# Input norm in two token halves, each followed by half of the first projection; the second layer reloads the transposed memory from DRAM

## The chip, the cores and the metric

The kernel runs on one core of one Trainium2 chip. The metric is device time in microseconds, median of three runs. Engines in the rows below: PE is TensorE (matmul), PEld its weight loads, DVE is VectorE, ACT is ScalarE, POOL is GpSimd, SP is SyncE, which issues most DMAs.

## The reference, cut to what matters

All of it is float32. `D_MODEL` is 1024, `SEQ` 512, `BATCH` 1, `DEPTH` 2, 256 memory tokens.

```python
def reference(x, mem, ln0_g, ln0_b, ...):
    h = layer_norm(x, ln0_g, ln0_b)                      # the input norm
    for l in range(DEPTH):
        mix = hybrid_mixer(h, w_in[l], ...)
        h = layer_norm(DEEPNORM_ALPHA * h + mix, ln1_g[l], ln1_b[l])
        xa = memory_cross_attention(h, mem, w_xq[l], w_xkv[l], w_xo[l])
        h = layer_norm(DEEPNORM_ALPHA * h + xa, ln2_g[l], ln2_b[l])
        ff = swiglu(h, w_ffn_in[l], w_ffn_out[l])
        h = layer_norm(DEEPNORM_ALPHA * h + ff, ln3_g[l], ln3_b[l])
    return h

def hybrid_mixer(h, w_in, ...):
    proj = h @ w_in                                      # c_a, c_g, q, k, v, r, a_low
    u = c_a * sigmoid(c_g)
    u = silu(layer_norm(causal_depthwise_conv(u, conv_w, conv_b), conv_ln_g, conv_ln_b))   # 31 taps
    ...
def memory_cross_attention(x, mem, w_q, w_kv, w_o):
    kv = mem @ w_kv                                      # mem: 256 x 1024, the same in both layers
    ...
```

## The kernel before, in words

A float32 operand is held as two fp32r tiles, a high part and the rest: `split` (L101) writes the high part with an ACT copy and the rest with a subtraction on DVE or POOL. `mm3` (L147) multiplies two such pairs with three matmuls (L148, L149, L150). Weights come in chunks of 512 KB: `wchunk` (L130) issues the load on SP into one of four `raw` buffers, then splits it into one of four `w` buffers (the ring). `wlo_engines` says which engine does the subtraction. After each such load, `behind` pops one waiting piece of work off the list `aside` and has it issued right after that load; before the change only `weight_sums`, later in each layer, puts anything there.

`proj_feat` (L223) computes a projection with features on the partitions: weights stationary, tokens moving, 512 of them in one matmul, or, with `halves`, 256 of them, first all matmuls of tokens 0 to 255 and then those of tokens 256 to 511, over the same four chunks.

The program starts with the memory: `mem_T` (L609) loads `mem` in four quarters, transposes each with four PE transposes, and splits the result into `mT` (two tiles of 128 x 2048 numbers, 1 MB each). `mem_V` (L638) makes V of layer 0 from it, K follows later in `mem_K`. Then comes the input norm (L665 to L684): statistics and the inverse deviation of four tiles of 128 tokens on DVE, the normalisation of each on ACT (L677), then for each of eight feature blocks four PE transposes into one PSUM bank (tag `tr`, two banks), an ACT step `xf` with gain and bias (L683), and a split into `hT`. The first projection on `hT` is `conv_in(0)` (L796), two groups of two chunks (`raw_c`, `w_c`, banks `pp_c`); `conv_taps` (L740) then runs 31 taps per channel tile on DVE at the lowest priority, `gates` (L754) comes between, and `conv_in(1)` is the other half of the channels. `residual0` multiplies and adds the gain and bias to `h` on POOL. In layer 1, `mem_T` is called again after `conv_in(0)`, since its tiles were given up in between.

The framework plans the program when it is built: it tracks the dependencies, hands out buffers, and orders each engine's instructions by priority (program order; `high_priority(offset=HP)` moves a block ahead) against its own estimate of times. So every engine has a fixed order of its own, and what stands later in the program can fill a gap. A small change of the text can move that order elsewhere too.

```python
    aside = []

    def behind(load):
        if aside:
            with tc.issue_after(load.ins):
                aside.pop(0)()
```

Of the kernel before, what the change touches and what calls it, by code (L numbers as in the profile page):

```python
# [12 lines left out]
F32 = mybir.dt.float32  # L13
# [38 lines left out]
def trunk(ctx: ExitStack, tc, a, out):  # L52
# [15 lines left out]
    def f(ap):  # L68
        return ap.bitcast(F32)
# [536 lines left out]
            dest.first(j, sg, uu)  # L606


    def mem_T(name):  # L609

        mT = [block([P, NK, MEM], F32R, f"mT{j}_{name}") for j in range(2)]
        mraws = block([P, 2, D], F32, f"mem_{name}")

        def part(*quarters):
            for mt, i in quarters:
                cs = slice(i * 512, i * 512 + 512)
                nc.sync.dma_start(mraws[:, mt, cs], a["mem"][0, mt * P:(mt + 1) * P, cs])
            for mt, i in quarters:
                pt = bank(f"mt{mt}{i}_{name}", tag="tr")
                for k in range(4):  # L620
                    PE.transpose(pt[:, k * P:(k + 1) * P], mraws[:, mt, (i * 4 + k) * P:(i * 4 + k + 1) * P], ident)
                ks, ms_ = slice(i * 4, i * 4 + 4), slice(mt * P, (mt + 1) * P)
                split(mT[0][:, ks, ms_], mT[1][:, ks, ms_], pt.rearrange("p (k t) -> p k t", k=4))

        return lambda kt: (mT[0][:, kt, :], mT[1][:, kt, :]), part

    def new_K(l):
        return [block([P, NK, MEM], F32R, f"KT{j}_{l}") for j in range(2)]
# [16 lines left out]
        for tt in tts:  # L645
            nc.sync.dma_start(h[tt], a["x"][0, tt * P:(tt + 1) * P, :])

    mT, mem_part = mem_T("0")
    mem_part((0, 0))
    lnrow = const.tile([2 * NK, P], F32, name="lnrow")  # L650
    V = new_V(0)
# [10 lines left out]
    DVE.tensor_copy(lncol, pl[:, :2 * NK])  # L662
    KT = new_K(0)
    hT = new_hT("ln0")
    with tc.high_priority(offset=HP):  # L665
        for tt in range(NT):
            st = ln_stats(tt, "ln0")
            for i in range(2):
                DVE.bn_stats(st[:, i, :], h[tt][:, i * 512:(i + 1) * 512])
            mv = small.tile([P, 2], F32, tag="mv", name=f"mv_ln0{tt}")  # L670
            DVE.bn_aggr(mv, st)
            v0 = small.tile([P, 1], F32, tag="v", name=f"v_ln0{tt}")
            DVE.tensor_scalar(v0, mv[:, 1:2], EPS, VS, ALU.add, ALU.mult)
            y0 = rstd_of(v0, 1, f"ln0{tt}")
            b0 = small.tile([P, 1], F32, tag="b0", name=f"b_ln0{tt}")
            DVE.scalar_tensor_tensor(b0, mv[:, 0:1], -1.0, y0, ALU.mult, ALU.mult)
            ACT.activation(h[tt], h[tt], AF.Identity, scale=y0, bias=b0)  # L677
        for k in range(NK):
            pt = bank(f"lt_ln0_{k}", tag="tr")
            for tt in range(NT):  # L680
                PE.transpose(pt[:, tt * P:(tt + 1) * P], h[tt][:, k * P:(k + 1) * P], ident)
            xf = tmp.tile([P, T], F32, tag="t", name=f"xf{k}")
            ACT.activation(xf, pt, AF.Identity, scale=lncol[:, k:k + 1], bias=lncol[:, NK + k:NK + k + 1])  # L683
            split(hT[0][k // 4][:, k % 4, :], hT[1][k // 4][:, k % 4, :], xf)  # L684

    gb0 = []

# [11 lines left out]
    for l in range(L):  # L699
# [30 lines left out]
        def conv_in(half):  # L730
            def ev_g(m, ps):
                ACT.activation(u[:, half * 2 + m, :], ps, AF.Sigmoid)

            def ev_a(m, ps):
                DVE.tensor_mul(u[:, half * 2 + m, :], u[:, half * 2 + m, :], ps)

            proj_feat(w_in, mov, [(CD + half * 256, 256, ev_g), (half * 256, 256, ev_a)], n_(f"c{half}"),
                      halves=half == 0 and l > 0)

        def conv_taps(half):  # L740
            cts = range(half * 2, half * 2 + 2)
# [12 lines left out]
        def gates():  # L754
# [38 lines left out]
            ACT.activation(kd, kd, AF.Exp, scale=1.0 / TAU)  # L793
            DVE.tensor_copy(dec, qe[:, :, CH - 1::CH])

        conv_in(0)  # L796
        if l == 0:
            residual0(0, 1)
        wlo_engines(POOL)
        if l > 0:  # L800
            mT, mem_part = mem_T(f"{l}")
            mem_part((0, 0), (1, 0), (0, 1), (1, 1))
            KT = new_K(l)
        conv_taps(0)
        gates()
# [288 lines left out]
```

## Time and profile before

| what | us |
|---|---|
| median of 3 runs | 1412.63 (1412.57 to 1413.6) |
| the profiled execution, its own time | 1414.95 |
| its span, first to last instruction | 1413.3 |
| around the span | 1.65 |

The profile is one execution. Durations below come from it, and a sum is made against its 1414.95 us, which is 2.32 us above the median. Matmuls are pipelined: the time from one start to the next is what PE needs, the duration shown is longer.

### The profile page before, as it was taken

The numbers are of one execution on the slowest core, as the hardware profiler recorded it, in microseconds if no ns is written. First come the engines' busy times: TensorE is split into PE (matmuls) and PEld (weight loads), VectorE is DVE, ScalarE is ACT, GpSimd is POOL, SyncE is SP. The second block draws the span as 40 slices with busy tenths as digits, with TensorE's granted clock in tenths as the row PEclk, the third lists the DMA queues.
The fourth block names the chain that finished last, engine by engine and source line by source line (L and its number), as shares of the span: only waits on it lengthen the run. The fifth ranks groups of instructions, "written<-read, shape, count | busy, mean of one in ns | idle before, by whom it ended". The sixth has DMA issues, their size and how long they took to land.

```text
span 1413.3 us, 22464 instructions
## 1 busy us (share of the span) xinstructions
PE 1380.2 (98%) x8847; PEld 1235.4 (87%) x8847; DVE 1110.4 (79%) x1905; ACT 650.4 (46%) x1065; POOL 181.8 (13%) x130
## 2 busy tenths in 40 slices
PE   7998999999999999999999999999999999999997
PEld 6687888988899899989888889889889998998996
DVE  6599978656988878877768999685579887878767
ACT  5652361343366456545235336524425653664550
POOL 2373331110000000001003300011100000000000
PEclk9999999999999999999999999999999999999998
DMA  7512247796255675565333225659913747646641
GB/s 255 154 60 87 93 148 196 203 259 164 75 134 142 193 174 150 165 193 134 122 111 103 75 90 179 227 140 275 223 60 107 180 136 204 176 138 204 154 134 60
DMA packets 131197, 214.79 MB, mean 152 GB/s; under 512 B 8956, under 2 KB 83408, under 8 KB 131092
## 3 DMA queue, kind: packets, MB, share of 16 engines
q1 hardware_dynamic: 118388, 175.35, 38.0%
q0 software_dynamic: 12416, 37.75, 14.6%
q8 instruction: 69, 1.13, 0.3%
q14 instruction: 36, 0.29, 0.1%
q10 hardware_dynamic: 288, 0.26, 0.1%
HBM read 190.27 MB, written 35.65 MB: 160 GB/s over the span
## 4 chain that ended last, share of the span: by engine, by line
PE 87%; DVE 3%; ACT 3%; issue 3%; POOL 2%; DMA 1%; SPq 0%; DVEq 0%; ACTq 0%; POOLq 0%
PE fx L551 5%; PE fx L553 5%; PE fx L552 5%; PE fw L553 3%; PE fw L552 3%; PE fw L551 3%; PE pp_xq L149 2%; PE pp_xq L148 2%; PE pp_xq L150 2%; PE foX_fo L512 2%; PE po_xo L150 2%; PE po_xo L148 2%; PE foX_fo L513 2%; PE po_xo L149 2%; PE foX_fo L514 2%
## 5 line engine op out<-in xcount | busy, mean ns | idle before, releaser
L750 DVE SCALAR_TENSOR_TENSOR cv<-u,chan,cv 128x511 f32<-128x511 f32 (+29 forms) x240 | 159.6, 728 | 0.2
L103 DVE TENSOR_TENSOR w_s<-s,w_s 128x1024 fp32r<-128x1024 f32 x80 | 97.6, 1220 | 38.9 <-ACT w_s L102 38.7
L306 POOL DMA_DIRECT2D s<-raw_a x40 | 34.8, 881 | 627.3 <-DVE h L495 187.1
L102 ACT ACTIVATE w_s<-s 128x1024 fp32r<-128x1024 f32 x80 | 84.5, 1056 | 66.5 <-DMA s<-raw_a 36.3
L551 PE MATMUL fx<-T_ln,w_s 128*128 128x256 f32 x320 | 90.6, 284 | 0.5 <-ACT u L564 0.5
L553 PE MATMUL fx<-T_ln,w_s 128*128 128x256 f32 x320 | 90.5, 283 | 0.0
L552 PE MATMUL fx<-T_ln,w_s 128*128 128x256 f32 x320 | 90.5, 283 | 0.0
L102 ACT ACTIVATE w_a<-raw_a 128x1024 fp32r<-128x1024 f32 x60 | 63.2, 1056 | 32.4 <-PE foX_fo L514 13.1
L103 DVE TENSOR_TENSOR w_a<-raw_a,w_a 128x1024 fp32r<-128x1024 f32 x60 | 73.1, 1219 | 5.0 <-ACT w_a L102 4.7
L551 PEld LDWEIGHTS fx<-T_ln,w_s 128*128 128x128 f32 x320 | 61.4, 192 | 0.9 <-ACT u L564 0.9
L552 PEld LDWEIGHTS fx<-T_ln,w_s 128*128 128x128 f32 x320 | 61.4, 192 | 0.0
L553 PEld LDWEIGHTS fx<-T_ln,w_s 128*128 128x128 f32 x320 | 61.4, 192 | 0.0
L149 PE MATMUL pp_xq<-hT_ln,w_xq 128*128 128x256 f32 (+1 forms) x192 | 61.3, 322 | 0.0
L148 PE MATMUL pp_xq<-hT_ln,w_xq 128*128 128x256 f32 (+1 forms) x192 | 59.9, 320 | 0.5 <-ACT hT_ln L102 0.5
L150 PE MATMUL pp_xq<-hT_ln,w_xq 128*128 128x256 f32 (+1 forms) x192 | 60.4, 318 | 0.0
L102 ACT ACTIVATE hT_ln<-lt_ln 128x512 fp32r<-128x512 f32 x24 | 13.9, 595 | 97.5 <-PE lt_ln L215 97.3
L149 PE MATMUL pp_c<-hT_ln,w_c 128*128 128x512 f32 (+1 forms) x160 | 56.9, 358 | 0.2 <-DVE hT_ln L103 0.2
L148 PE MATMUL pp_c<-hT_ln,w_c 128*128 128x512 f32 (+1 forms) x160 | 55.1, 361 | 1.7 <-DVE h L295 1.5
L150 PE MATMUL pp_c<-hT_ln,w_c 128*128 128x512 f32 (+1 forms) x160 | 56.3, 354 | 0.0
L102 ACT ACTIVATE w_S_fo<-raw_S_fo 128x1024 fp32r<-128x1024 f32 x32 | 33.8, 1058 | 35.8 <-PE foX_fo L514 14.2
L149 PE MATMUL po_xo<-w_xo,oTh 128*128 128x512 f32 x128 | 49.5, 389 | 0.0
L150 PE MATMUL po_xo<-w_xo,oTl 128*128 128x512 f32 x128 | 49.4, 391 | 0.0
(369 smaller groups left out, 4869.2 us busy)
## 6 DMA issues: line engine op xcount, KB each, us to landing
raw_a<-w_ffn_in SPq DMA_DIRECT2D x60, 512.0 KB, 4.1
s<-raw_a POOLq DMA_DIRECT2D x40, 512.0 KB, 5.6
raw_fo<-w_ffn_out SPq DMA_DIRECT2D x36, 512.0 KB, 3.9
S_fs<-w_ffn_out SPq DMA_DIRECT2D x32, 512.0 KB, 6.4
raw_S_fo<-S_fs SPq DMA_DIRECT2D x32, 512.0 KB, 3.7
s<-w_ffn_in SPq DMA_DIRECT2D x20, 512.0 KB, 3.4
raw_xv<-w_xkv SPq DMA_DIRECT2D x16, 512.0 KB, 5.7
raw_c<-w_in SPq DMA_DIRECT2D x16, 512.0 KB, 4.7
```

The source lines that it names most:

```text
L102: ACT.activation(hi, src, AF.Copy)
L103: eng.tensor_sub(lo, src, f(hi))
L148: PE.matmul(o, lh, rh, start=start, stop=False)
L149: PE.matmul(o, lh, rl, start=False, stop=False)
L150: PE.matmul(o, ll, rh, start=False, stop=stop)
L306: POOL.dma_start(dst, src, accum_op=ALU.add, max_dma_last_dim=4096)
L512: PE.matmul(o, ph[:, ts_], wh, start=first, stop=False, skip_group_check=True)
L513: PE.matmul(o, ph[:, ts_], wl, start=False, stop=False, skip_group_check=True)
L551: PE.matmul(o, wh, bh, start=start and k == 0, stop=False, skip_group_check=True)
L552: PE.matmul(o, wh, bl, start=False, stop=False, skip_group_check=True)
L553: PE.matmul(o, wl, bh, start=False, stop=stop and k == 3, skip_group_check=True)
L750: DVE.scalar_tensor_tensor(cv[ct][:, s:], u[:, ct, :T - s], wj, cv[ct][:, s:], ALU.mult, ALU.add)
```

## The change

The input norm becomes a function of a token half: statistics, normalisation, transposes and splits of tiles 0 and 1, then of tiles 2 and 3. A PSUM bank holds two feature blocks of 256 tokens instead of one of 512, with one `xf` step for each and one split for both. `conv_in(0)` runs in token halves in layer 0 too. In layer 0 the two `mT` tiles are written to DRAM (`mdram`), each behind one of the weight loads of `conv_in(0)`; in layer 1 two POOL DMAs read them back, in place of the loads, transposes and splits of `mem_T`.

```diff
+    mdram = [dram.tile([P, NK, MEM], F32, tag=f"mT{j}", name=f"mT{j}_dram") for j in range(2)]
+
+    def mem_views(mT):
+        return lambda kt: (mT[0][:, kt, :], mT[1][:, kt, :])
+
+    def mem_again(l):
+
+        mT = [block([P, NK, MEM], F32R, f"mT{j}_{l}") for j in range(2)]
+        for j in range(2):
+            POOL.dma_start(mT[j], mdram[j])
+        return mem_views(mT)
...
     hT = new_hT("ln0")
-    with tc.high_priority(offset=HP):
-        for tt in range(NT):
+    def input_norm(t):
+        tts = range(t * 2, t * 2 + 2)
+        for tt in tts:
             st = ln_stats(tt, "ln0")
...
             ACT.activation(h[tt], h[tt], AF.Identity, scale=y0, bias=b0)
-        for k in range(NK):
-            pt = bank(f"lt_ln0_{k}", tag="tr")
-            for tt in range(NT):
-                PE.transpose(pt[:, tt * P:(tt + 1) * P], h[tt][:, k * P:(k + 1) * P], ident)
-            xf = tmp.tile([P, T], F32, tag="t", name=f"xf{k}")
-            ACT.activation(xf, pt, AF.Identity, scale=lncol[:, k:k + 1], bias=lncol[:, NK + k:NK + k + 1])
-            split(hT[0][k // 4][:, k % 4, :], hT[1][k // 4][:, k % 4, :], xf)
+        s = slice(t * 256, t * 256 + 256)
+        for k2 in range(NK // 2):
+            pt = bank(f"lt_ln0_{t}{k2}", tag="tr")
+            xf = tmp.tile([P, T], F32, tag="t", name=f"xf{t}{k2}")
+            for e in range(2):
+                k, es = k2 * 2 + e, slice(e * 256, e * 256 + 256)
+                for i, tt in enumerate(tts):
+                    PE.transpose(pt[:, e * 256 + i * P:e * 256 + (i + 1) * P], h[tt][:, k * P:(k + 1) * P], ident)
+                ACT.activation(xf[:, es], pt[:, es], AF.Identity, scale=lncol[:, k:k + 1],
+                               bias=lncol[:, NK + k:NK + k + 1])
+            k4 = k2 * 2 % 4
+            split(hT[0][k2 // 2][:, k4:k4 + 2, s], hT[1][k2 // 2][:, k4:k4 + 2, s],
+                  xf.rearrange("p (e c) -> p e c", e=2))
+
+    with tc.high_priority(offset=HP):
+        for t in range(2):
+            input_norm(t)
...
             proj_feat(w_in, mov, [(CD + half * 256, 256, ev_g), (half * 256, 256, ev_a)], n_(f"c{half}"),
-                      halves=half == 0 and l > 0)
+                      halves=half == 0)
...
+        if l == 0:
+            for j in range(2):
+                aside.append(lambda j=j: nc.sync.dma_start(mdram[j], f(mT_tiles[j])))
         conv_in(0)
         if l == 0:
             residual0(0, 1)
         wlo_engines(POOL)
         if l > 0:
-            mT, mem_part = mem_T(f"{l}")
-            mem_part((0, 0), (1, 0), (0, 1), (1, 1))
+            mT = mem_again(l)
             KT = new_K(l)
         conv_taps(0)
```

## Rows read from the trace of the kernel before

**Rows 1.** The page: the span, and busy time, share of the span and instructions of each engine.

```profile
span 1413.3 us, 22464 instructions
PE 1380.2 (98%) x8847; PEld 1235.4 (87%) x8847; DVE 1110.4 (79%) x1905; ACT 650.4 (46%) x1065; POOL 181.8 (13%) x130
```

**Rows 2.** What PE waited for in the whole run, longest in total first: us in total, times, longest.

```profile
PE mt L621 <- DMA mem<-mem: 6.2, 2, 4.1
PE lt_ln L681 <- ACT xf L683: 3.4, 1, 3.4
PE pt_v L149 <- POOL w_v L103: 1.9, 1, 1.9
PE ogt L954 <- DVE og L950: 1.8, 1, 1.8
```

**Rows 3.** PE in order of time around the input norm and `conv_in(0)` of layer 0: start, duration, instruction, count, and in brackets the idle time before it.

```profile
35.33 0.60 PE L681 MATMUL lt_ln<-ident,h 128*128 128x128 f32 x4
39.34 1.70 PE L681 MATMUL lt_ln<-ident,h 128*128 128x128 f32 x8 [3.41 <-ACT xf L683]
40.69 2.06 PE L148 MATMUL pp_c<-hT_ln,w_c 128*128 128x512 f32 x4
42.97 0.63 PE L150 MATMUL pp_c<-hT_ln,w_c 128*128 128x512 f32 x1
43.39 0.47 PE L149 MATMUL pp_c<-hT_ln,w_c 128*128 128x512 f32 x1
...
61.57 0.39 PE L148 MATMUL pp_c<-hT_ln,w_c 128*128 128x512 f32 x1
...
66.10 0.39 PE L150 MATMUL pp_c<-hT_ln,w_c 128*128 128x512 f32 x1
66.33 3.86 PE L770 MATMUL al<-hT_ln,wa 128*32 128x512 f32 x16
```

**Rows 4.** Stretches of that time: us, PE, PEld, DVE, ACT and POOL busy, the granted clock of PE (1.00 is 2.4 GHz), the busy share of the DMA engines, GB/s.

```profile
30.00:32.00 2.00, 2.00 (x11) 1.65 (x10) 0.77 (x7) 1.82 (x2) 0.13 (x1) 1.00 0.91 261
32.00:34.00 2.00, 2.00 (x12) 1.63 (x11) 0.00 (x0) 2.00 (x3) 0.00 (x0) 1.00 1.00 339
36.00:38.00 2.00, 0.00 (x0) 0.00 (x0) 2.00 (x2) 2.00 (x3) 0.00 (x0) 1.00 0.00 0
40.00:42.00 2.00, 2.00 (x7) 1.80 (x8) 1.19 (x2) 1.38 (x2) 0.00 (x0) 0.54 0.51 80
```

**Rows 5.** ACT in order of time, from the normalisation of the four tiles on.

```profile
30.18 4.64 ACT L677 ACTIVATE h<-h,b_ln,y_ln 128x1024 f32<-128x1024 f32 x4 [4.04 <-DVE b_ln L676]
34.73 1.99 ACT L102 ACTIVATE w_c<-raw_c 128x1024 fp32r<-128x1024 f32 x2
36.62 0.57 ACT L102 ACTIVATE V<-pt_xv 128x512 fp32r<-128x512 f32 x1
37.10 1.04 ACT L102 ACTIVATE w_c<-raw_c 128x1024 fp32r<-128x1024 f32 x1
38.05 0.57 ACT L102 ACTIVATE V<-pt_xv 128x512 fp32r<-128x512 f32 x1
38.52 1.43 ACT L683 ACTIVATE xf<-lt_ln,lncol 128x512 f32<-128x512 f32 x2
```

**Rows 6.** SP in order of time: the four loads of `conv_in(0)` in layer 0.

```profile
27.75 9.68 SPq L134 DMA_DIRECT2D raw_c<-w_in  x4
```

**Rows 7.** DMA in the window 1404 to 1413 us, the last stores of the output from SBUF to DRAM: GB/s in 40 equal slices.

```profile
GB/s 0 0 0 0 0 0 0 0 0 0 0 0 0 0 46 337 391 364 383 410 355 46 0 0 0 0 114 341 223 350 342 337 332 287 5 0 0 0 0 0
```

**Rows 8.** Layer 1, PE: `conv_in(0)` in halves, and then the transposes of the memory.

```profile
724.12 0.28 PE L148 MATMUL pp_c<-hT_ln,w_c 128*128 128x256 f32 x1
...
726.88 0.29 PE L148 MATMUL pp_c<-hT_ln,w_c 128*128 128x256 f32 x1
...
745.24 1.04 PE L621 MATMUL mt<-ident,mem 128*128 128x128 f32 x8
746.04 3.96 PE L770 MATMUL al<-hT_ln,wa 128*32 128x512 f32 x16
749.83 0.40 PE L148 MATMUL pp_c<-hT_ln,w_c 128*128 128x512 f32 x1
...
752.80 0.60 PE L621 MATMUL mt<-ident,mem 128*128 128x128 f32 x4
753.16 0.47 PE L149 MATMUL pp_c<-hT_ln,w_c 128*128 128x512 f32 x1
```

**Rows 9.** PE: the transposes of the memory in both layers, and in layer 1 the first of the three lines that read `mT` for K (count; ns, least, median, most; first and last start).

```profile
L621 PE MATMUL mt<-ident,mem x32: 270/273/476, 4.1 to 754.0; 128*128 128x128 f32 x32
...
L148 PE MATMUL pp_xk<-mT,w_xk x64: 278/283/387, 818.7 to 870.7; 128*128 128x256 f32 x64
```

**Rows 10.** The tile `S_fs` in DRAM: the POOL instruction that issues a DMA of 512 KB (ns, least, median, most), and the us to landing of the DMAs that write it, from DRAM to DRAM.

```profile
L306 POOL DMA_DIRECT2D S_fs<-S_fs x16: 814/840/1372, 231.1 to 1017.7; - x16
DMA to landing us min/median/max: 3.2/8.0/9.9
```

**Rows 11.** Layer 0, POOL in order of time, behind `conv_in(0)`.

```profile
65.72 9.50 POOL L693 TENSOR_TENSOR h<-h,gb_ln 128x1024 f32<-128x1024 f32 x4
75.17 2.42 POOL L103 TENSOR_TENSOR w_c<-raw_c,w_c 128x1024 fp32r<-128x1024 f32 x1
77.53 9.48 POOL L694 TENSOR_TENSOR h<-h,gb_ln 128x1024 f32<-128x1024 f32 x4
86.98 7.10 POOL L103 TENSOR_TENSOR w_qk<-raw_qk,w_qk 128x1024 fp32r<-128x1024 f32 x3
```

**Rows 12.** DVE: one addition of `gates` in layer 0 and in layer 1; ACT: the copy of the first conv half, ahead of the `w_v` split of the wait in rows 2.

```profile
85.20 9.95 DVE L785 TENSOR_TENSOR qk<-qk 128x1024 f32<-128x1024 f32 x1 [2.50 <-ACT qk L784]
769.40 1.23 DVE L785 TENSOR_TENSOR qk<-qk 128x1024 f32<-128x1024 f32 x1 [2.96 <-ACT qk L784]
123.86 0.60 ACT L752 ACTIVATE acc<-cv 128x512 f32<-128x512 f32 x1 [13.76 <-DVE cv L750]
```

**Rows 13.** What PE waited for from 700 to 910 us, as in rows 2: the end of layer 0 and the mixer of layer 1.

```profile
PE pp_c L148 <- DVE h L295: 1.5, 1, 1.5
PE pu L839 <- DVE S L851: 0.4, 1, 0.4
```

More of the change, by code (lines that the diff above doesn't have):

```diff
@@ L623, in part @@
                 split(mT[0][:, ks, ms_], mT[1][:, ks, ms_], pt.rearrange("p (k t) -> p k t", k=4))
-        return lambda kt: (mT[0][:, kt, :], mT[1][:, kt, :]), part
+        return mT, part
     def new_K(l):
@@ L646, in load_x @@
             nc.sync.dma_start(h[tt], a["x"][0, tt * P:(tt + 1) * P, :])
-    mT, mem_part = mem_T("0")
+    mT_tiles, mem_part = mem_T("0")
+    mT = mem_views(mT_tiles)
     mem_part((0, 0))
```

## Prediction, made before the changed kernel was run

> **What bounds the kernel now.** I read the page first: PE is busy for 1380.2 of 1413.3 us [rows 1], so only two things can shorten this kernel, PE work that goes and PE idle time that goes. Then the list of PE's waits, because it says where the 33 us of idle time lie. The largest, 6.2 us, is the first load of the memory, which the change doesn't touch. The second is the one place the change aims at: 3.4 us before a transpose of the input norm, waiting for ACT's `xf` [rows 2].
>
> The order of time shows how that wait comes about. V's matmuls end at about 35.3, the eight transposes among and behind them fill both banks, and from 35.93 PE has nothing until 39.34 [rows 3]. ACT did not idle: four tile normalisations from 30.18 to 34.8, then three weight splits and two V copies, and only at 38.52 the first `xf`, which frees a bank [rows 5]. So PE waits for ACT's queue. [...] Eight transposes then took 1.35 us (39.34 to 40.69) against 0.80 us for eight at full clock in layer 1 [rows 3, 8], and the matmuls up to 43.39 came about 0.43 us apart (42.97 to 43.39), where the same form later takes 0.227 (20 intervals from 61.57 to 66.10) [rows 3]. From 40.69 to 43.39 there are 6 matmuls, so the clock cost 0.55 + 6 x 0.20 = 1.75 us.
>
> **The change part by part.**
>
> *The wait and the clock.* With the norm in halves, the first `xf` needs two tile normalisations on ACT, not four. Each takes about 1.15 us (4.64 for four, [rows 5]), and the statistics of tiles 0 and 1 no longer queue behind those of 2 and 3. The transposes of half 0 can then run while V's matmuls still last. If hT of half 0 is ready when V ends, PE goes on without a gap: 3.41 us of wait and 1.75 us of clock are gone, 5.16 in all. I don't take all of it: at 36 to 38 us ACT is busy the whole time [rows 4], and weight splits and V copies still want 5 us of it around that point [rows 5]. ACT also gets 16 `xf` steps of half the columns for 8 whole ones; a whole one takes about 0.7 (1.43 for two, [rows 5]), so 8 more cost between nothing and 5.6 us of ACT, nearer 2 if half a step saves less than half. They lie beside PE's first pass of 11.5 us. I leave 1.0 us of wait: -4.2.
>
> *The halves.* 96 matmuls of 512 tokens become 192 of 256. Layer 1 shows their pace: 724.12 to 726.88 are 23 intervals of 0.120 us [rows 8]. A pair takes 0.240 for 0.227: 96 x 0.013 = +1.3 us. The number of input transposes stays at 32, the splits at 8. The ring's four chunks are now held into the second pass. Layer 1 already works that way, and PE goes from the last half (745.24) through 16 gate matmuls to the next projection at 749.83 without a gap [rows 8]; cost 0. Head in sum: -4.2 + 1.3 = -2.9; at best -5.16 + 1.3 = -3.9, at worst +1.3 with the wait kept.
>
> *The two stores.* 2.10 MB from SBUF to DRAM on SP's queue, one behind the first and one behind the second weight load. Nothing in `mT` is late for them. Output stores move 337 to 410 GB/s in their full slices, about 370 [rows 7], so 5.7 us of DMA time; by the rate of the weight loads themselves, 261 to 339 [rows 4], 6 to 8 us. What is queued behind: chunks 2, 3 and 4 of `conv_in(0)`. Before, the first three are issued from 27.75 on and loaded by about 34 us [rows 4, 6]. With the stores between, the third lands at about 34 + 5.7 = 40 and is split some 2.2 us later (1.04 ACT [rows 5], then as much again for the subtraction): 42. PE, if it starts the first pass at 36.5, uses a chunk in 24 x 0.12 = 2.9 us and wants the third at 42.3. So it is just hidden, by the first two chunks' work. If the stores are slower, the planner has 5.8 us of second-pass work on the first two chunks to put there. I take 0.
>
> [...]
>
> *Layer 1.* Four loads of 256 KB on SP, 16 transposes, four ACT copies and four DVE subtractions go. PE: eight transposes take 745.24 to 746.04, 0.80; a group of four takes 0.36 plus about 0.08 at the change of form, twice: 0.8 + 0.9 = -1.7 us [rows 8]. From 700 to 910 us PE's largest wait is 1.5 us for the layer before, and the next 0.4 [rows 13]; nothing takes the gain back, so all of it counts. ACT's and DVE's relief is off the path: 0. In its place two POOL instructions, 0.84 us each by the nearest one [rows 10] (for 512 KB; here 1 MB, so 0.8 to 1.7 each), and 2.10 MB of reads. K, the first reader, starts at 818.7 [rows 9], over 70 us after `conv_in(0)` ends. Even 10 us to landing, the most that a DMA of that kind took [rows 10], is hidden. Behind them in POOL's queue stand the subtractions of `conv_in(1)`'s chunks; if the planner puts the reads ahead of these, they are late by 2 to 3 us against 4.6 us of gate matmuls. 0, at worst +3.
>
> *Sum:* -2.9 - 1.7 = -4.6 us. The profiled execution's 1414.95 becomes 1410.3; the median's 1412.63 becomes **1408.0**.
>
> **The rivals.**
>
> *B: the head's gain is eaten later in layer 0.* PE waits 1.9 us for `w_v` near 125.5 [rows 2]. That chunk's ACT split stands behind the copy of the first conv half, which waited 13.76 us for DVE's taps [rows 12]. The taps share DVE with one addition that took 9.95 us in layer 0 and 1.23 in layer 1; in layer 0 it ran from 85.2 to 95.15, under POOL's unbroken run that ends at 94.08 [rows 11, 12]. If POOL's run, which begins with the residual at 65.72 when its gain and bias have landed, doesn't come earlier with `conv_in(0)`, DVE is held until the same moment, the taps end at the same 123.9, and PE waits there for what it gained. Then only layer 1 counts: -1.7, 1410.9. For it: POOL is behind from 65.7 to 94 [rows 11]. Against it: that run waits for chunk splits and a load whose places in the queues move with PE.
>
> *C, slower: the stores hold the weights.* Its place is SP's queue at 28 us. The third chunk is ready at 34 + 2 stores + 2.2 and PE, after the first two chunks (42.3) and their second pass (+5.8), stands still from 48.1: it decides from 6 us a store, and since the other terms give 5.16 - 1.3 + 1.7 = 5.6 us back, the kernel is slower than before from 8.8 us a store. DMAs of 512 KB that write DRAM took 8.0 us to land in the median [rows 10], so 16 for 1 MB at the worst; at 12, the middle between that and the point where it turns, the chunk is ready at 60.2, PE stands 12.1 us, loses 1.75 to the clock again, and the sum is 12.1 + 1.75 - 5.6 = +8.3: 1420.9. For it: the loads queue behind the stores. Against it: rows 10 are DRAM to DRAM in a busy stretch, rows 7 are the direction in question, 2.8 us a store.
>
> *D: a transpose holds PE for as long as it lasts.* One lasts 0.273 us [rows 9]; 16 of them would be 4.4 us, 2.7 more than I count, and the time 1405.3. Against it: the trace starts them 0.10 us apart, since they overlap [rows 8]. [...]
>
> *E: the plan moves.* All engines' orders are planned anew. Waits like those of 1.5 to 1.9 us [rows 2] can appear or vanish anywhere in layer 0: -4 to +5 around the forecast.
>
> **How the numbers follow.** Forecast (1405 to 1410): 0.50. B (1410 to 1412.5): 0.22. C (1415.5 to 1424): 0.10. D (1405): 0.02. E on its own, outside these: 0.16, of which 0.04 below 1405, 0.06 about as before, 0.06 slower. 0.2% of 1412.6 is 2.8 us, about what a measurement here tells from no change. Faster by more: 0.50 + 0.06 + a little of B = 0.58. Within: most of B and 0.06 of E, 0.27. Slower: C and the rest of E, 0.15. For 8 in 10, the range runs from 1403.5 to 1414.5: below lies part of E's low end, above it C and part of E.
>
> **What would show it.** The wait of PE for `xf` near 36 us falls from 3.4 to about 1 us and the clock stays at 1.00 at 36 to 44 us. `conv_in(0)` ends, and the gate matmuls start, near 63 instead of 66.33. The `pp_c` matmuls of layer 0 are 256 wide and 0.120 apart. No `mt` transpose after 20 us, and K's first matmul in layer 1 comes without a wait for a DMA. B would show as a longer wait at `pt_v` with POOL's run still ending at 94; C as ACT waiting for `raw_c` at 36 to 60 us. I would be wrong most plainly if PE's idle time at the head grew.

## The result, and the profile after

The changed kernel takes 1415.61 us in the median of 21 runs (1413.72 to 1420.21), the kernel before 1413.61 in 21 runs beside them: a ratio of 1.0017, 95% interval 1.0010 to 1.0024. It is some 2.4 us slower; I had forecast 1408.0 in a range up to 1414.5. By the prediction's own 0.2% it is "within", at the edge to "slower"; "faster", which had the largest chance, did not come. The profiled execution of after took 1418.09 us, 3.1 more than that of before.

The page of after, its span and busy times, for [rows 1]:

```profile
span 1416.4 us, 22624 instructions
PE 1381.0 (98%) x8927; PEld 1241.3 (88%) x8927; DVE 1104.4 (78%) x1901; ACT 652.6 (46%) x1070; POOL 187.4 (13%) x132
```

PE's busy time grew by 0.8 us (96 more matmuls, 16 fewer transposes) and its idle time by 2.3. The list of PE's waits of after says where that is, for [rows 2]:

```profile
PE mt L633 <- DMA mem<-mem: 6.4, 2, 3.9
PE ogt L980 <- DVE og L976: 3.8, 1, 3.8
PE lt_ln L699 <- ACT xf L700: 2.9, 2, 1.7
PE po_mo L150 <- DVE cUl L103: 2.4, 2, 1.3
PE pp_qk L148 <- DVE u L759: 2.1, 1, 2.1
```

The wait for `xf`, which the change was to shorten, is 2.9 us instead of 3.4, now in two parts. The waits at `pt_v` are gone, and three have come or grown in layer 0's mixer, all three for DVE: `u` (the gated input of the convolution), `og` (the gated attention output) and `cUl` (the low part of the convolution's output, which the mixer's output projection `po_mo` reads).

**The head.** PE of after in order of time, for [rows 3]:

```profile
37.21 0.89 PE L699 MATMUL lt_ln<-ident,h 128*128 128x128 f32 x4 [1.27 <-ACT xf L700]
39.77 0.89 PE L699 MATMUL lt_ln<-ident,h 128*128 128x128 f32 x4 [1.66 <-ACT xf L700]
40.75 0.74 PE L148 MATMUL pp_c<-hT_ln,w_c 128*128 128x256 f32 x2
...
68.10 2.25 PE L794 MATMUL al<-hT_ln,wa 128*32 128x512 f32 x9
```

The first `pp_c` starts at 40.75 (before: 40.69), the gate matmuls `al` at 68.10 (before: 66.33). ACT in the same stretch, for [rows 5]:

```profile
30.63 4.65 ACT L691 ACTIVATE h<-h,b_ln,y_ln 128x1024 f32<-128x1024 f32 x4 [4.04 <-DVE b_ln L690]
35.18 1.04 ACT L102 ACTIVATE w_c<-raw_c 128x1024 fp32r<-128x1024 f32 x1
36.13 0.57 ACT L102 ACTIVATE V<-pt_xv 128x512 fp32r<-128x512 f32 x1
36.61 1.01 ACT L700 ACTIVATE xf<-lt_ln,lncol 128x256 f32<-128x256 f32 x2
37.71 1.06 ACT L102 ACTIVATE w_c<-raw_c 128x1024 fp32r<-128x1024 f32 x1
38.68 0.58 ACT L102 ACTIVATE V<-pt_xv 128x512 fp32r<-128x512 f32 x1
39.16 1.02 ACT L700 ACTIVATE xf<-lt_ln,lncol 128x256 f32<-128x256 f32 x2
40.06 0.64 ACT L102 ACTIVATE hT_ln<-xf 128x512 fp32r<-128x512 f32 x1
```

The source has two halves, ACT's queue does not: the plan put all four normalisations first, and the weight splits and V copies between the `xf` pairs. The first cast to `hT`, on which `pp_c` waits, comes at 40.06. The clock falls as it did before; stretches of after, columns as in [rows 4] (the clock as a share of full speed; no trace here gives it in GHz):

```profile
36.00:38.00 2.00, 0.77 (x4) 0.40 (x4) 1.74 (x2) 1.90 (x5) 0.00 (x0) 1.00 1.07 445
40.00:42.00 2.00, 1.90 (x10) 1.45 (x9) 1.62 (x4) 2.00 (x5) 0.00 (x0) 0.71 1.07 293
42.00:44.00 2.00, 2.00 (x11) 2.00 (x11) 0.83 (x2) 2.00 (x4) 0.00 (x0) 0.50 0.19 45
```

**Layer 1.** PE of after behind the first half of the convolution, for [rows 8]; then, for [rows 9], the memory's transposes in the whole run and the reload (count; ns, least, median, most; first and last start):

```profile
749.84 3.87 PE L794 MATMUL al<-hT_ln,wa 128*32 128x512 f32 x16
753.55 0.40 PE L148 MATMUL pp_c<-hT_ln,w_c 128*128 128x512 f32 x1
```

```profile
L633 PE MATMUL mt<-ident,mem x16: 364/421/476, 3.9 to 13.4; 128*128 128x128 f32 x16
L618 POOL DMA_DIRECT2D mT<-mT_dram x2: 552/570/587, 745.1 to 745.7; - x2
```

No transpose of the memory stands there any more, and K has no wait. After was 4.6 us behind before when layer 1 began (first `pp_c` of each trace, 720.69 against 716.11), 3.8 at `al` and 2.7 at the first `pp_qk`: 1.9 us given back. The clock falls once in this stretch in both traces (0.50 at 724 to 726 us in after, at 720 to 722 in before). e2 and e4 (below), where it does not fall there, differ by the same 1.9 us (55.5 and 53.6 us from the first `pp_c` to `pp_qk`).

Between head and layer 1 the distance to before runs like this: +1.8 at `al`, +4.0 at the end of `pp_qk` (the mixer's q and k), -2.1 at the end of `pt_v` (its v), +4.2 at the first `po_mo`, +6.7 at `pp_xq` (the first projection behind the mixer), +4.6 at the end of layer 0. So the 3.1 us between the two traces are 1.8 at the head, another 2.8 in the rest of layer 0, -1.9 in layer 1 up to `pp_qk` and 0.4 behind it. The mixer of layer 0, for which my sum had no term, decides.

### The profile page after: what moved, and what is told of

The parts are those of the page before. It is cut to its first block, busy times and chain, and to the rows that moved or that the text cites. A ratio compares the mean times of both kernels' runs of the same rounds, so it can differ in the third digit from the quotient of the medians.

```text
span 1416.4 us, 22624 instructions
## 1 busy us (share of the span) xinstructions
PE 1381.0 (98%) x8927; PEld 1241.3 (88%) x8927; DVE 1104.4 (78%) x1901; ACT 652.6 (46%) x1070; POOL 187.4 (13%) x132
## 4 chain that ended last, share of the span: by engine, by line
PE 87%; DVE 8%; ACT 2%; DMA 1%; issue 1%; SPq 0%; DVEq 0%; ACTq 0%
PE fx L551 5%; PE fx L553 5%; PE fx L552 5%; DVE cv L774 3%; PE fw L553 3%; PE fw L552 3%; PE fw L551 3%; PE pp_xq L148 2%; PE pp_xq L149 2%; PE pp_xq L150 2%; PE po_xo L150 2%; PE foX_fo L512 2%; PE foX_fo L513 2%; PE po_xo L148 2%; PE po_xo L149 2%; PE pp_c L149 2%
## 5 line engine op out<-in xcount | busy, mean ns | idle before, releaser
L774 DVE SCALAR_TENSOR_TENSOR cv<-u,chan,cv 128x511 f32<-128x511 f32 (+28 forms) x240 | 158.9, 729 | 0.1
L149 PE MATMUL pp_c<-hT_ln,w_c 128*128 128x256 f32 (+1 forms) x192 | 62.6, 329 | 0.2 <-DVE hT_ln L103 0.2
L148 PE MATMUL pp_c<-hT_ln,w_c 128*128 128x256 f32 (+1 forms) x192 | 60.8, 328 | 1.8 <-DVE h L295 1.5
L150 PE MATMUL pp_c<-hT_ln,w_c 128*128 128x256 f32 (+1 forms) x192 | 62.1, 327 | 0.0
```

Of the source, the lines that this page charges most:

```text
L148: PE.matmul(o, lh, rh, start=start, stop=False)
L149: PE.matmul(o, lh, rl, start=False, stop=False)
L150: PE.matmul(o, ll, rh, start=False, stop=stop)
L774: DVE.scalar_tensor_tensor(cv[ct][:, s:], u[:, ct, :T - s], wj, cv[ct][:, s:], ALU.mult, ALU.add)
```

## The experiments

All ratios are to the kernel before, in runs taken beside it; 0.1% is 1.4 us.

| kernel | median us | ratio (95%) |
|---|---|---|
| after | 1415.61 | 1.0017 (1.0010 to 1.0024) |
| e1 reload alone | 1410.47 | 0.9985 (0.9971 to 0.9999) |
| e2 halves alone | 1418.60 | 1.0036 (1.0025 to 1.0047) |
| e3 norm halved, projection whole | 1416.78 | 1.0028 (1.0015 to 1.0041) |
| e4 late stores | 1416.82 | 1.0025 (1.0013 to 1.0037) |
| e5 after, mixer's splits on DVE | 1410.48 | 0.9975 (0.9962 to 0.9988) |
| e6 after, half 0 first on ACT | 1417.37 | 1.0026 (1.0015 to 1.0038) |
| e7 after, gain loaded early | 1409.93 | 0.9979 (0.9969 to 0.9988) |
| e8 = e1 + e5's edit | 1407.48 | 0.9960 (0.9948 to 0.9972) |
| e9 = e6 + late stores | 1418.56 | 1.0033 (1.0020 to 1.0045) |
| e10 = e9 + e5's and e7's edits | 1410.10 | 0.9972 (0.9961 to 0.9982) |
| e11 = e1 + e5's and e7's edits | 1403.39 | 0.9925 (0.9908 to 0.9941) |
| e12 = after + e5's and e7's edits | 1408.48 | 0.9951 (0.9932 to 0.9969) |
| e13 = e9, splits behind `xf` | 1418.98 | 1.0035 (1.0022 to 1.0049) |
| e14 = e13 + e5's and e7's edits | 1407.99 | 0.9962 (0.9950 to 0.9974) |
| e15 = before + e5's and e7's edits | 1407.13 | 0.9955 (0.9940 to 0.9971) |
| e16 = e9, splits behind `hT` | 1415.94 | 1.0012 (1.0000 to 1.0024) |
| e17 = e16 + e5's and e7's edits | 1402.01 | 0.9925 (0.9909 to 0.9941) |

### Which part of the change costs

e1 is the kernel before with the stores and the reload; e2 the changed kernel with layer 1's transposes back and no stores; e3 and e4 are the changed kernel with one edit each:

```diff
 e3:
-                      halves=half == 0)
+                      halves=half == 0 and l > 0)
 e4 (the two stores, queued ahead of conv_in(1) instead of conv_in(0)):
+        gates()
+        if l == 0:
+            for j in range(2):
+                aside.append(lambda j=j: nc.sync.dma_start(mdram[j], f(mT_tiles[j])))
         conv_in(1)
```

> The kernel before with the second half of the change alone: the two stores behind the loads of conv_in(0) in layer 0 and the reload in layer 1; input norm and conv_in(0) as before. Theory 1 (layer 1 gains its 1.7 us, and what the change loses is lost in layer 0 by the halves): about 1.9 us faster than before, with conv_in(0) of layer 0 ending at the same 66 us. Theory 2 (the stores hold the weights of conv_in(0)): ACT waits for raw_c, conv_in(0) ends 2 us or more later, and the whole is at the time of before or up to 3 us slower.

> The changed kernel without stores and reload: layer 1 transposes the memory again. Theory 1 (the halves cost layer 0 some 4 us): about 4 us slower than before, 1417 to 1418. Theory 2 (the stores do): conv_in(0) starts earlier than 40.7 us and ends before 66 us, and the whole is 0 to 3 us faster than before.

> The changed kernel with one part undone: conv_in(0) of layer 0 runs over all 512 tokens at once again, the input norm stays in halves. If the 256 wide matmuls are the loss at the head (96 pairs of 0.240 for 0.227 us), conv_in(0) ends 1.3 us earlier than in the changed kernel and the whole is about 1.3 us faster than it. If the halves of the projection are what lets PE start, PE waits longer before conv_in(0) (its first matmul then needs both halves of hT), and the whole is slower than the changed kernel by 3 us or more.

> The changed kernel with the two stores behind the first two loads of conv_in(1) instead of conv_in(0). If the stores hold the weights of conv_in(0), its last two chunks come 3 to 6 us earlier, and conv_in(0) ends 1 to 3 us earlier than 68.1. If ACT's queue alone sets the start, conv_in(0) ends at 68 as before and the time stays within 1 us of the changed kernel.

The reload brings 2.1 us (0.1 to 4.1), the halves cost 5.1 (3.5 to 6.6); 0.9985 x 1.0036 = 1.0021, the change's 1.0017 within the intervals. So the loss is the halves'. In e3 the first `pp_c` starts 6.3 us later than in before and `al` 4.9 later: the halved projection does let PE start while half 1 is not there, but that only makes good what the halved norm alone would cost. In e4 `al` comes 3.0 us later than in before, against 1.8 in after: moving the stores away did not bring the head forward, and rival C falls. These distances hold a part that is the clock's: at the head it was at half from 40.1 to 43.6 us in before (0.50 at 41 to 43), twice as long in e4 and three times as long in e3, in part while PE waited.

### What holds the mixer of layer 0

The chain of work that ended last runs in after, from 90 to 149 us, almost wholly over DVE: the gates' steps and the convolution's taps. In before it runs from 80 to 128 us over POOL: the residual, then the splits of `w_qk` and `w_v`, with gaps between them. Two stretches (columns as in [rows 4]), first before, then e17:

```profile
90.00:110.00 20.00, 20.00 (x89) 16.33 (x88) 20.00 (x23) 7.16 (x8) 10.85 (x5) 1.00 0.39 117
110.00:150.00 40.00, 36.30 (x205) 29.92 (x204) 39.99 (x65) 11.46 (x17) 16.20 (x8) 0.96 0.32 99
```

```profile
90.00:110.00 20.00, 20.00 (x90) 16.57 (x89) 20.00 (x30) 7.10 (x7) 8.94 (x5) 1.00 0.36 110
110.00:150.00 40.00, 40.00 (x246) 33.31 (x245) 39.96 (x69) 14.10 (x19) 18.05 (x8) 1.00 0.35 106
```

The columns are, after the window's length, PE, PEld, DVE, ACT, POOL: in before DVE is busy for 20.00 of 20 and 39.99 of 40 us. That alone does not hold PE. In e17 DVE is as busy, and so is PE, for all of the 60 us: the taps have the lowest priority and fill what DVE has left. What holds PE is a single DVE step that comes late when PE needs its result. And DVE's busy time is not all work. DVE of after, from the gates on, and POOL beside it:

```profile
90.08 1.97 DVE L809 TENSOR_TENSOR qk<-qk 128x1024 f32<-128x1024 f32 x1 [3.96 <-ACT qk L808]
93.27 5.39 DVE L811 TENSOR_TENSOR_SCAN dk<-reset,qk 128x512 f32<-128x512 f32 x2
99.85 2.09 DVE L815 TENSOR_TENSOR dk<-dk 128x1024 f32<-128x1024 f32 x1
101.86 0.68 DVE L759 TENSOR_TENSOR u<-u,pp_c 128x512 f32<-128x512 f32 x1
```

```profile
88.54 2.44 POOL L103 TENSOR_TENSOR w_qk<-raw_qk,w_qk 128x1024 fp32r<-128x1024 f32 x1
90.91 3.40 POOL L718 TENSOR_TENSOR h<-h,gb_ln 128x1024 f32<-128x1024 f32 x1
94.27 6.59 POOL L103 TENSOR_TENSOR w_qk<-raw_qk,w_qk 128x1024 fp32r<-128x1024 f32 x2
```

The addition takes 1.97 us where it takes 1.23 undisturbed [rows 12]: it starts at 90.08, POOL's split ends at 91, and it is done 1.1 us later. So the last of the three: POOL's splits end at 100.86, and it too is done 1.1 us later. The two scans between them also end 1.1 us after the POOL step in which each began (95.39 after 94.31, 98.66 after 97.58). The taps between these steps, which add up in a PSUM bank, keep their 0.73 us beside the same POOL work. Why the one kind of step waits for POOL and the other does not, no trace here shows. `u` frees the bank that `pp_qk` waits for.

The wait for `og` is of this kind too, and here before and after differ in what was held. In after two small DVE steps ahead of `og` stood beside POOL splits, from 177.74 to 180.15 and from 182.33 to 184.28 us; in before only the first did, and the wait was 1.8 us instead of 3.8. During the longer wait the clock fell, and it is at half from 184 to 191 us in after (0.51 in the mean).

e5 takes POOL's part in the mixer's second group of splits away, e7 makes POOL's run earlier (`gb0` holds the gain and bias of the residual):

```diff
 e5:
         if l == 0:
-            wlo_engines(POOL, DVE)
+            wlo_engines(DVE)
 e7:
+        if l == 0:
+            gb0.append(load_gb(a["ln0_g"], a["ln0_b"], "ln0"))
         conv_in(0)
```

> The changed kernel, where from the second chunk pair of K in layer 0 on (up to the output projection of the mixer) all weight subtractions are done by DVE, not by POOL and DVE in turn. Theory H (a DVE instruction that reads and writes only SBUF stands still while a POOL instruction runs, and that is what the mixer's end loses): the waits for cUl and cUh before po_mo (3.6 us) and for og (3.8 us) shrink to 2 us or less together, and the whole is 3 to 5 us faster than the changed kernel. Theory O (the loss there is DVE's own work, in another order): with more work on DVE the waits grow, and the whole is 0 to 4 us slower than the changed kernel.

> The changed kernel with the load of the input norm's gain and bias for the residual issued ahead of conv_in(0)'s loads in program order. If POOL's run of residual and weight subtractions starts when that load has landed, it starts before 69.7 us, ends before 100.9, DVE's steps of gates and the product u are not held, the wait of pp_qk for u (2.1 us) goes, and the whole is 2 us or more faster than the changed kernel. If POOL's run waits for something else (the chunks' splits), it starts at 69 to 70 as before and nothing moves by over 1 us.

> Experiment e1 (the reload alone, 0.15% faster than before) with the edit of e5. Theory H: another 2 to 4 us faster, as the kernel before has the same waits at the mixer's end, for og 1.8 and before po_mo 1.5 us: about 0.3 to 0.4% faster than before. Theory O: the same as e1 or slower.

e5 is 5.9 us faster than after, e7 5.4. In e7 the load is issued at 42.02 instead of 63.62 and POOL's unbroken run ends at 76.8 instead of 100.86. DVE of e7, the same four steps:

```profile
89.55 1.23 DVE L809 TENSOR_TENSOR qk<-qk 128x1024 f32<-128x1024 f32 x1 [3.95 <-ACT qk L808]
91.98 3.25 DVE L811 TENSOR_TENSOR_SCAN dk<-reset,qk 128x512 f32<-128x512 f32 x2
96.43 1.21 DVE L815 TENSOR_TENSOR dk<-dk 128x1024 f32<-128x1024 f32 x1
97.56 0.67 DVE L759 TENSOR_TENSOR u<-u,pp_c 128x512 f32<-128x512 f32 x1
```

From the addition to `u` it is 8.0 us instead of 11.8; the three steps account for it (5.69 against 9.45), and PE's wait for `u` is gone. For e5, the two subtractions that the `cUl` wait stands for, in after with POOL beside them, and in e5:

```profile
211.65 5.26 DVE L103 TENSOR_TENSOR cUl<-csl,cUh 128x512 fp32r<-128x512 f32 x2 [0.35 <-ACT cUh L102]
```

```profile
211.18 5.18 POOL L103 TENSOR_TENSOR w_mo<-raw_mo,w_mo 128x1024 fp32r<-128x1024 f32 x2 [10.65 <-ACT w_mo L102]
```

```profile
209.37 0.69 DVE L103 TENSOR_TENSOR cUl<-csl,cUh 128x512 fp32r<-128x512 f32 x1 [0.15 <-ACT cUh L102]
210.05 0.68 DVE L103 TENSOR_TENSOR cUl<-csl,cUh 128x512 fp32r<-128x512 f32 x1
```

Beside POOL's two splits (211.18 to 216.36) they took 2.6 us each, without them 0.69. PE's waits for `og`, `cUl` and `cUh` are gone in e5, though it moves seven more splits of 1.2 us onto DVE. Its wait for `u` grew, from 2.1 to 5.2 us, since the plan moved there too; the whole is faster in spite of it. (The profiled execution of e5 is its slowest, 1414.59 us.) e8 adds e5's edit to e1: 0.9960 for 0.9985.

At `u` the holds alone don't tell before from after: in before the addition alone lost 8.7 us [rows 12], more than all three steps in after. There PE did not yet need `u`, and paid at `pt_v` instead. A wait of PE for `u`, 2.1 to 7.3 us in sum, stands in every trace that has the projection halved and the gain loaded late (after, e2, e4, e5, e6, e9, e13, e16) and in no other: not with e7's edit, not without halves, not in e3. In these traces the wait comes with the halved projection and goes with the early gain. Why the plan then asks for that bank sooner is not shown.

### Whether the head's gain was there to be had

```diff
 e6 (in input_norm; last_xf holds the last xf of half 0):
+            if last_xf:
+                with tc.issue_after(last_xf[0]):
+                    ACT.activation(h[tt], h[tt], AF.Identity, scale=y0, bias=b0)
 e9: e6, and the stores as in e4
 e13, e16 (in wchunk, the chunks 2 to 4 of conv_in(0) in layer 0), on e9:
+                with tc.issue_after(hold[...]):
+                    split(w[:, 0, c0:c0 + step], w[:, 1, c0:c0 + step], raw[:, c0:c0 + step], eng)
 e13: hold is the second pair of xf; e16: the first hT cast, for chunks 3 and 4 the second
```

> The changed kernel with the normalisation of tiles 2 and 3 held behind the last xf step of tiles 0 and 1 in ACT's order; nothing else asked for. If the four normalisations ahead of the first xf are what keeps PE waiting at the head, the first pp_c comes 2.3 us earlier than 40.75 (two normalisations of 1.15 us), PE's wait for xf falls from 2.9 to 1 us or less and conv_in(0) ends near 65.5. If DVE's chain (b at 30.6 us) and the two banks of the transposes set it, the first pp_c moves by less than 1 us.

> The changed kernel, with the normalisations of tiles 2 and 3 put behind the last xf of half 0 on ACT (as in the run before this one) and the two stores moved behind the loads of the convolution's second half. Theory 'two queues': the first xf of half 0 has two things ahead of it on ACT, the four normalisations and the weight split of a chunk whose load is queued on SP behind a 1 MB store; with both gone PE's wait for xf falls from 2.9 us to under 1.5 us, the first pp_c starts near 38 instead of 40.75 us, the clock reads 1.00 sooner, and the gate matmuls start near 65 instead of 68.1. Rival 'ACT is full': V copies and splits still take the time, the wait stays at 3 us and the first pp_c near 40. For the whole run the first theory still expects only 0 to 3 us less than the changed kernel, since DVE and POOL set the mixer's tail.

> The run with half 0 first on ACT and the stores late, and with the weight splits of chunks 2, 3 and 4 of the convolution's first half put behind the second pair of xf steps. Theory 'ACT's order': three splits of 1.05 us no longer stand ahead of the first four xf and the first hT split; PE's wait for xf falls from 4.1 us to under 1.5 us, the first pp_c starts near 37 instead of 40.5 us, and the gate matmuls start at 65 to 66 instead of 68.5. Then PE may wait for chunk 2 instead, 1 to 2 us. Rival 'the bound is elsewhere' (V copies, PE's own transposes, DVE's subtractions): the first pp_c stays at 40 or later. The whole run stays at 1414 to 1418, since the mixer's tail is as it was.

> The run with half 0 first on ACT and the stores late, and with the weight split of chunk 2 put behind the first hT step on ACT and those of chunks 3 and 4 behind the second: the order that the prediction assumed. Theory 'ACT's order': the first pp_c starts at about 36.5 us, 4 us sooner than in the changed kernel, and PE waits for xf, hT and chunks 3 us less in sum by the gate matmuls (65 to 66 us). Rival 'ACT is full': xf, hT steps and splits of half 0 take some 8 us of ACT in all between 32 and 42 us, PE starts sooner but waits 3 us for chunk 2 and the later hT steps, and the gate matmuls stay at 67 to 68. In both the whole run stays at 1414 to 1418, by the mixer's tail.

In e6 two normalisations come first, and something else is late. ACT of e6:

```profile
34.78 1.01 ACT L706 ACTIVATE xf<-lt_ln,lncol 128x256 f32<-128x256 f32 x2
37.56 1.06 ACT L102 ACTIVATE w_c<-raw_c 128x1024 fp32r<-128x1024 f32 x1 [1.77 <-DMA raw_c<-w_in]
```

The first `xf` come 1.8 us sooner, but ACT then waits 1.77 us for a chunk whose load was issued behind the first store, and the next `xf` stand behind that split. PE waits 3.3 us, the first `pp_c` starts at 40.59. In e9 the store is out of the way too, and the first `pp_c` starts at 40.51: ACT runs three weight splits ahead of the first `xf` (4.1 us of waits). In e13 these are behind the `xf`, whose wait falls to 0.5 us, but then ahead of the first cast. PE and ACT of e13:

```profile
39.26 1.22 PE L153 MATMUL pp_c<-hT_ln,w_c 128*128 128x256 f32 x4 [2.91 <-ACT hT_ln L102]
```

```profile
35.73 2.96 ACT L102 ACTIVATE w_c<-raw_c 128x1024 fp32r<-128x1024 f32 x3
38.58 0.63 ACT L102 ACTIVATE hT_ln<-xf 128x512 fp32r<-128x512 f32 x1
```

In three steps out of three the next item of the same queue took over the wait. Only e16 has the order that my prediction had taken for granted. ACT, then PE and two stretches of e16:

```profile
33.59 1.02 ACT L713 ACTIVATE xf<-lt_ln,lncol 128x256 f32<-128x256 f32 x2 [0.43 <-PE lt_ln L712]
34.51 0.59 ACT L102 ACTIVATE V<-pt_xv 128x512 fp32r<-128x512 f32 x1
34.98 1.03 ACT L713 ACTIVATE xf<-lt_ln,lncol 128x256 f32<-128x256 f32 x2
35.88 0.65 ACT L102 ACTIVATE hT_ln<-xf 128x512 fp32r<-128x512 f32 x1
36.40 1.08 ACT L102 ACTIVATE w_c<-raw_c 128x1024 fp32r<-128x1024 f32 x1
```

```profile
35.61 0.90 PE L712 MATMUL lt_ln<-ident,h 128*128 128x128 f32 x4 [0.51 <-ACT xf L713]
36.59 0.50 PE L155 MATMUL pp_c<-hT_ln,w_c 128*128 128x256 f32 x2
```

```profile
38.00:40.00 2.00, 1.83 (x16) 1.63 (x15) 1.90 (x3) 2.00 (x3) 0.00 (x0) 1.00 0.06 6
40.00:42.00 2.00, 2.00 (x19) 2.00 (x18) 1.84 (x3) 1.90 (x4) 0.00 (x0) 1.00 0.50 59
```

The first `pp_c` starts at 36.59, the granted clock reads 1.00 in every stretch from 34 to 46 us, `al` comes at 63.62, 2.7 us before the kernel before. Not all of this is the order's: V's last matmul starts at 33.96 in this trace and at 35.09 in before. From there to the first `pp_c` it is 2.6 us instead of 5.6. Nor is the clock sure: e17 has the same order and the same waits up to there, and in its trace the clock fell at 37.6 us (0.50 at 38 to 40) and `al` comes at 65.14.

The gain is lost again in the mixer: PE waits 3.7 us for `u`, the clock is at half from 99 to 106 us (0.83 in the mean of 90 to 110), and at `kdt` (the transposes behind `pp_qk`) e16 is 4.0 us behind before. The whole run is 1.0012.

### Both together

> The kernel of the run before with two more edits: gain and bias of the residual loaded before the convolution's first half, and the mixer's second group of weight splits on DVE instead of POOL and DVE. If the halves of the norm are good in themselves and lose only to POOL's runs beside DVE, this one keeps the head's gain to the end of layer 0: about 1404 to 1406 us, under the reload alone with the tail on DVE (0.996 of the kernel before). If the halves cost more than they bring, it ends at 1408 to 1411.

> No halves: the kernel before with the stores and the reload, the gain and bias loaded early and the mixer's second group of splits on DVE. Theory 'POOL holds DVE': the early load took 5.4 us off the changed kernel because POOL's unbroken run then ends about 24 us sooner; here PE has no wait for u at pp_qk to lose, so at most the waits at pt_v and pu (1.6 us each) go: 0 to 3 us under the same kernel without the early load, 1404.5 to 1407.5.

> The changed kernel as it is, with both edits (gain and bias early, the mixer's second group of splits on DVE). Each alone took 5.4 to 5.9 us off the changed kernel. If they act in two places (u at pp_qk and the residual's run; og, cUl and cUh in the tail), they add up in part: 1405 to 1408. If both only move the same wait, it stays at about 1410.

> The same with gain and bias early and the mixer's second group of splits on DVE, so that neither ACT's order at the head nor POOL's runs hold the halves back. If the halves are worth anything, this is at or under the version without halves with the same two edits (0.9925 of the kernel before, 1403.4 us). If the order of the head gains 3 us and the halves cost 1.3 us of PE and what the later loads lose, it lands at 1405 to 1408.

> The kernel before, without the change, with the two edits alone (gain and bias early, the mixer's second group of splits on DVE). If the reload is worth the 1.7 us of transposes here as in the prediction, this is 1405 to 1406, some 2 us over the version with the reload; the two edits then carry most of the 11 us that version gained.

> The same with gain and bias early and the mixer's second group of splits on DVE. If the head's gain then reaches the end: 1403 to 1405, level with the version without halves (0.9925 of the kernel before). If a gain at the head is lost again in layer 0, or there is none: 1407 to 1408, as with the splits behind xf (0.9962).

With e5's and e7's edits in all of them, the order of ACT at the head decides what the halves are worth: e12 (the change as made) 0.9951, e10 0.9972, e14 0.9962, e17 (the assumed order) 0.9925. Without halves it is 0.9925 as well (e11), with neither halves nor reload 0.9955 (e15). e14 and e17 differ only in where three splits stand in ACT's queue, and their intervals lie apart: with the POOL holds out of the way this order is worth 0.37% to the halves, 5.2 us, and brings them level with no halves, not ahead. Against e12 the gain is 3.7 us, but these intervals overlap, and e17 also has the stores late. In the profiles e17 is 1.6 us ahead of e11 at `al` and 4.3 at the end, but e11's profiled execution was its slowest (1406.37), so no difference between the two is shown. e10 took the worse of its two branches: its first `pp_c` starts at 40.95 and `al` at 72.70 (e9: 40.51 and 68.52), with waits for `xf` and `hT` and the clock at half up to 46 us (0.50 at 40 to 46) and again at 60 to 63 (0.61 in the mean of 60 to 64), which is most of what it loses to e9 there. e11 and e17 came out 1 us under their expectations, e12 half a us and e15 1 us over, e14 in the worse of its branches; e9 and e13 came out slower than expected as a whole (1418.56 and 1418.98). The reload is worth 4 us between e15 and e11, but the intervals of the two, measured at different times, touch.

e11 and e17 are the fastest, 0.75% under the kernel before; the three lines of e5 and e7 alone (e15) bring 0.45%, with none of the change under study.

## Why the prediction was wrong, point by point

**The wait and the clock (-4.2), wrong for this kernel.** The failed sentence is "the first `xf` needs two tile normalisations on ACT, not four". Needed, yes; but ACT's queue is ordered by the plan, and it kept four in a row and put splits and V copies between the `xf` pairs. PE's wait for `xf` went from 3.4 to 2.9 us instead of 1.0, and the clock fell again. I had seen the splits and copies in [rows 5] (they add up to 4.2 us there, not 5) and left 1.0 us for them by choice. The statistics of tiles 0 and 1 did not come forward either: in after and in e16 DVE has the shifts `b_ln` of all four tiles ready within 0.7 us, and the first normalisation starts behind the first of them, at 30.63 us in after (30.18 in before).

The term's size was near. From before to e16, with the assumed order, PE's waits up to `al` fell by 2.4 us, as forecast, and the clock did not fall. Where it can be compared, a fall cost less than the 1.75 us that I took: in layer 1 the stretch from the first `pp_c` to `pp_qk` takes 55.1 us with a fall (after, e16) and 53.6 without (e1, e4). That `al` came at 63.62 there ("near 63") is in part luck: V ended 1.1 us sooner, and in e17, with the same order, the clock fell again.

**The halves (+1.3), right in kind.** The matmuls are 256 wide and 0.120 us apart; from first `pp_c` to `al` after takes 27.35 us, before 25.64: +1.7, with four transposes in it that in before ran ahead of the first `pp_c`.

**The stores (0), right.** In after ACT waited 0.1 us for `raw_c` at the head. The cover was real: e6 took it away, and 1.8 us of wait appeared: that load was issued at 30.97 us, behind the first store, and ACT's wait for it ended at 37.56, 6.6 us later, where the one load of the first 60 us whose landing the profile of before has took 4.3. So a load behind a store came later in e6, by about 2 us and not by the 6 to 12 us a store of rival C. Whether the order of the queue or the shared DMA engines made it late is not shown.

**Layer 1 (-1.7), right.** 0.8 at the first group and 1.1 at the others, 1.9 in all; e1 gives 2.1 by itself. Rival D falls with it: 16 transposes did not cost 4.4 us.

**What had no term.** I read [rows 1] as "only PE work and PE idle time can shorten this kernel" and summed from the head to the end as if layer 0's mixer passed a gain on or left things as they were. There PE waits for single DVE steps, some of which stand still under POOL, and which of them are caught changes with the plan: after lost 2.8 us between `al` and the end of layer 0, and e16 lost more than its gain. Rival B had the place and the mechanism, POOL's run under DVE, with a chance of 0.22; it was taken only as "the gain is eaten". The run did not end at 94 but at 100.86: its gain and bias load went out at 63.62 instead of 58.42. The convolution's transposes `pc` ran at 60.67 instead of 56.99, their rows hold a slot of the same buffers, and the last chunk's load and this one stand behind it on SP. That last link is read from the trace; e7, which takes the load out of that queue place, agrees with it but does not show it alone.

**E, the plan moves.** It did: -2.1 us at `pt_v`, and another 2.1 given back in layer 0's FFN, of which PE's waits there explain 0.8 (1.0 before, 0.2 after). Where the rest comes from stays open.

## What to carry over

Before an idle gap of the busiest engine is counted as gain, follow the chain behind it to the next step of another engine that it will need, and ask whether that step can come sooner; if it can't, the gain ends there. That the other engine is busy all the time does not decide it: it can be busy with work that can wait. When work is cut in halves, write down the order in which each queue will run the pieces, and force it if the gain hangs on it: here moving three 1 us splits (e13 to e16) brought the first matmul 2.7 us forward. And the SBUF-only steps shared out to POOL were not free for DVE here: the addition of the gates took 9.95 us under POOL's run and 1.23 without it [rows 12]. Count how long DVE's own steps stand still beside such a run.

## What the runs showed of the hardware

Most DVE instructions on SBUF alone stood still while POOL added, multiplied or subtracted. In after, 15 steps that read and wrote SBUF alone, wider than 128x1, started while a POOL step ran that had more than 0.1 us to go; 13 of them took 0.4 to 2.3 us longer than their like without POOL. Even small ones did: a scaling of 128x2 elements at 198.15 us took 2.42 us beside a POOL split (198.13 to 200.53), where the like take 0.16 to 0.17. Not all did: two subtractions at 221.84 and 222.44 took 0.68 us as without POOL, and of the steps on 128x1 elements inside a POOL split (27.20 to 30.57) those that start between 28.24 and 29.70 us took 0.20 to 0.26 us each, as they do alone, while the next, at 29.82, took 0.77 for 0.14. Steps with a PSUM bank were not held: the taps that add up took 0.71 to 0.75 us beside POOL in after, within 0.02 us of the same form without it. POOL's steps lengthened too: its two splits from 94.27 took 6.59 us, where single ones at 67.32 and 79.11 took 2.41 and 2.44.

A store of 1 MB from SBUF took 7.3 us from issue to landing in after (one of the two has its landing in the profile; 6.9 to 7.9 in the other runs with the stores at the head), some 2.6 times the 2.8 that I took from the rate in [rows 7]. ACT's wait for the loads behind the stores was 0.1 us in after and 1.8 in e6. The two reads of 1 MB in layer 1 took 6.9 and 8.9 us.

The same waits did not bring the same clock: in e16 and e17 PE waits 0.5 us at 35.6 and 0.2 at 37.3, and the clock fell at 37.6 us in e17 alone. Such a fall cost 1.5 us in layer 1 (55.1 against 53.6, above), and e16 and e17 reach `al` 1.5 us apart (63.62 and 65.14) after the same waits up to the fall.
